# Recurrent gates of a Griffin encoder: both input parts stacked along the rows, gate halves moved by transfers

## The chip, the cores and the metric

The kernel runs on one core of a Trainium2 chip. The metric is the device time of one execution in microseconds (us). Times of a kernel are medians of several runs; the profile is one further execution, taken with the hardware profiler.

TensorE (PE) multiplies, VectorE (DVE), ScalarE (ACT) and GpSimd (POOL) do the rest, and nearly all transfers are issued by one queue, SyncE's (SP). PE accumulates into PSUM, which has eight banks of 128 x 512 float32 here.

## What is computed

Two layers, each a half-step FFN, a mixer, and a second half-step FFN, over 512 tokens of width 1024. The mixer projects once and runs attention beside a recurrent branch; the change touches the gates of that branch alone:

```python
def rg_lru(x, wa, ba, wx, bx, lam, reverse):
    xb = x.reshape(b, s, N_RNN_BLOCKS, RNN_BLOCK)             # 16 blocks of 64 channels
    r = sigmoid(einsum('bsnc,ncd->bsnd', xb, wa) + ba)
    i = sigmoid(einsum('bsnc,ncd->bsnd', xb, wx) + bx)
    log_a = -LRU_C * r * softplus(-lam)
    a = exp(log_a)
    u = sqrt(-expm1(2.0 * log_a)) * (i * x)
    _, h = associative_scan(_lin_combine, (a, u), axis=1, reverse=reverse)
    return h

hr = rg_lru(xc, ..., False) + rg_lru(xc, ..., True)           # xc: the convolved input
rnn = (hr * gelu(yr)) @ w_rnn_o
```

Every weight matrix of a gate is block diagonal: 16 blocks of 64 x 64 per gate and direction.

## The kernel before, in words

**Precision.** Every product of two float32 operands is built from float32r parts. An operand is split into a high part (ACT copies it to float32r) and a low part (DVE subtracts), and `mm3` (line 320) adds three matmuls: high by high, low by high, high by low.

**Layout.** Channels lie on partitions, tokens (512) along the free dimension. 1024 channels are eight tiles c = 0 to 7 of 128 channels, so that a tile holds two 64-channel blocks of the recurrence.

**Order.** The order is written by hand. `mix_ops` (line 176) lists the mixer's operations; `step()` (line 143) ticks a program clock, once per six matmuls in most operations, and `later(n, f)` puts the instructions of f into the engines' queues n ticks on. An engine runs its queue in order and waits only for its data, so a lag sets who stands ahead of whom and is no delay in itself. Every tick may also start a unit of attention (`unit`, line 732: two score banks, softmax, and two transposing DMAs of the probabilities on SP); a `pv` (line 783) follows every fourth unit.

**Weights.** `next_w()` (line 311) hands out weight chunks (128 x 512 float32, a gate's chunk 128 x 256) in program order. Its load goes out about ten chunks ahead on SP, its split into high and low about six chunks ahead on ACT and DVE. Chunks named in `EARLY` are split long before they are needed: `presplit` (line 231), during the layer's first FFN, loads a chunk, splits it, and writes both parts to the DRAM buffer `lsave`, from where `load_to` (line 279) later fetches both parts ready for use. It starts at tick `EARLY_AT[0]` of that FFN and takes a new chunk every `EARLY_AT[1]` ticks. Before, 72 chunks of each layer go this way, and the gates' chunks (`lru0`, `lru1`) do not.

**The recurrence.** `conv` (line 848) makes the tile `xc` and its parts `xh` (ACT) and `xl` (DVE). `lru(c, d)` (line 875), for direction d, takes two PSUM banks, one per gate: bank 0 for r, bank 1 for i, each `mm3` of a 128 x 128 weight with two 64 x 64 blocks on its diagonal. That is six matmuls and one tick. `tr` takes the tanh of each bank into the tiles `tr` and `ti` (one ACT instruction each, which frees the bank); `de` makes the decay `a` and the tanh of r on ACT and multiplies i by `xc` on DVE. After the second direction `rt` takes the square roots and `recur` (line 909) runs products, scans, sum and split. `R_LAGS` holds the lags: tr 1, de 2, rt 5. The last tile, c = 7, is the last that the output projection of the branch (`rnn`) waits for.

All SBUF work tiles come from one pool of 95 tiles.

Of the kernel before, what the change touches and what calls it, by code (L numbers as in the profile page):

```python
# [9 lines left out]
F32R = mybir.dt.float32r  # L10
F16 = mybir.dt.float16
ACTF = mybir.ActivationFunctionType
ALU = mybir.AluOpType
# [5 lines left out]
KD = D // 128  # L19
# [11 lines left out]
GELU_K = 0.7978845608028654  # L31
GELU_C = 0.044715


KC = 4

# [11 lines left out]
G_LAGS = (1, 2, 4, 6)  # L48
U_LAGS = (1, 5, 7, 9, 11, 14)
R_LAGS = (1, 2, 5, 1, 2, 6, 9, 13, 15)  # L50
GATES_1 = (1, 1, 1, 1, 1, 0, 0, 0)
GATES_2 = (1, 1, 1, 1, 1, 1, 0, 0)
GATES_3 = 1
# [8 lines left out]

EARLY = {"gA": 8, "gB": 8, "yr": 8, "xr": 8, "ao": 8}
EARLY_AT = (30, 3)
RATES = {"kv": 0.0, "q": 0.33, "xr": 0.33, "gA": 0.33, "gB": 0.33, "yr": 0.33, "lru0": 0.3, "lru1": 0.3, "rnn": 0.6, "aoa": 0.6, "ao": 0.0, "wk": 0.0, "wo": 0.0}


# [1 line left out]
def tile_griffin_encoder(  # L71
# [19 lines left out]
    V, A, G, SP, PE = nc.vector, nc.scalar, nc.gpsimd, nc.sync, nc.tensor  # L91
# [15 lines left out]
    def T(p, dtype=F32, shape=(128, 512)):  # L107
        return pool.tile(list(shape), dtype, name=nm(p), tag="T")

    def PS():  # L110
        return psp.tile([128, 512], F32, name=nm("ps"), tag="ps")
# [4 lines left out]
    def act(out, in_, func, **kw):  # L116
        A.activation(out, in_, func, **kw)  # L117

    def tt(out, a, b, op):
        V.tensor_tensor(out=out, in0=a, in1=b, op=op)  # L120
# [10 lines left out]
    def f32(ap):  # L131
        return ap.bitcast(F32)
# [6 lines left out]
    def later(n, fn):  # L139
        clock[1] += 1  # L140
        heapq.heappush(pend, (clock[0] + n, clock[1], fn))
# [13 lines left out]
    chunks = []  # L155
# [75 lines left out]
    def presplit(l, t0, dt):  # L231

        for n, i in enumerate(early[l]):
            st = {}

            def ld(i=i, st=st):
                ap, cols = chunks[i]
                st["w"] = T("er")
                SP.dma_start(out=st["w"].rearrange("p (a b) -> p a b", a=ap.shape[1]), in_=ap)

            def hi(st=st):
                st["h"] = T("eh", F32R)
                act(st["h"], st["w"], ACTF.Copy)

            def lo(st=st):
                tt(st["w"], st["w"], f32(st["h"]), ALU.subtract)

            def out(i=i, n=n, st=st):
                SP.dma_start(out=lsave[n, 0], in_=f32(st["h"]))
                SP.dma_start(out=lsave[n, 1], in_=st["w"])  # L250
                lows[i] = (lsave[n, 0], lsave[n, 1])

            for d, f in ((0, ld), (5, hi), (6, lo), (9, out)):
                later(t0 + n * dt + d, f)
# [24 lines left out]
    def load_to(n):  # L279
        while pos[0] < min(n, len(chunks)):  # L280
            ap, cols = chunks[pos[0]]
            if pos[0] in lows:
                hl = T("wh", F32R), T("wl", F32R)
                for t, src in zip(hl, lows[pos[0]]):
                    SP.dma_start(out=f32(t), in_=src)
                loaded[pos[0]] = hl
            else:
                t = T("wr")
                dst = t[:, 0:cols]
                if len(ap.shape) == 3:  # L290
                    dst = dst.rearrange("p (a b) -> p a b", a=ap.shape[1])
                SP.dma_start(out=dst, in_=ap)
                loaded[pos[0]] = t
            pos[0] += 1
# [25 lines left out]
    def mm3(ps, wh, wl, xh, xl, start, stop):  # L320
        PE.matmul(ps, wh, xh, start=start, stop=False)  # L321
        PE.matmul(ps, wh, xl, start=False, stop=False)  # L322
        PE.matmul(ps, wl, xh, start=False, stop=stop)  # L323
# [225 lines left out]
    def mix(l, norm, v, on_x):  # L549
        p = prm_t[l]  # L550
        hb, hc, nhc, sc, tb = v["hb"], v["hc"], v["nhc"], v["sc"], v["tb"]
        h = norm.h
# [295 lines left out]
        def conv(c, ps):  # L848
            st = rst[c] = {}
            xc = T("xc")  # L850
            st["xc"] = xc

            def w(j):
                return p[:, P_CW + 4 * c + j:P_CW + 4 * c + j + 1]

            act(xc, ps, ACTF.Identity, scale=w(2), bias=p[:, P_CB + c:P_CB + c + 1])

            def cj(o, i, j):
                stt(xc[:, o], ps[:, i], w(j), xc[:, o], ALU.mult, ALU.add)

            def ch():
                st["xh"] = T("xh", F32R)
                act(st["xh"], xc, ACTF.Copy)

            def cl():
                st["xl"] = T("xl", F32R)
                tt(st["xl"], xc, f32(st["xh"]), ALU.subtract)

            later(1, lambda: cj(slice(2, S), slice(0, S - 2), 0))
            later(1, lambda: cj(slice(1, S), slice(0, S - 1), 1))  # L870
            later(2, lambda: cj(slice(0, S - 1), slice(1, S), 3))
            later(3, ch)
            later(4, cl)

        def lru(c, d):
            st = rst[c]
            wh, wl = next_w()
            ps = []
            for g in range(2):
                ps.append(PS())  # L880
                sl = slice(g * 128, (g + 1) * 128)
                mm3(ps[g], wh[:, sl], wl[:, sl], st["xh"], st["xl"], True, True)
            step()
            j = d * 8 + c

            def tr():
                for n, q in enumerate(("r", "i")):
                    t = st[q, d] = T("t" + q)
                    act(t, ps[n], ACTF.Tanh, scale=0.5, bias=hb[:, 16 * n + j:16 * n + j + 1])

            def de():
                a, r = T("a"), st["r", d]
                st["a", d] = a
                act(a, r, ACTF.Exp, scale=hc[:, j:j + 1], bias=hc[:, j:j + 1])
                act(r, r, ACTF.Tanh, scale=nhc[:, j:j + 1], bias=nhc[:, j:j + 1])
                stt(st["i", d], st["i", d], 1.0, st["xc"], ALU.add, ALU.mult)

            later(R_LAGS[0], tr)
            later(R_LAGS[1], de)
            if d == 1:  # L900

                def rt():
                    for e in range(2):
                        act(st["r", e], st["r", e], ACTF.Sqrt, scale=0.25)

                later(R_LAGS[2], rt)
                recur(c, R_LAGS[2])

        def recur(c, t0):
            st = rst[c]  # L910
# [215 lines left out]
def _layout(inputs):  # L1126
    import numpy as np

    i = {k: np.asarray(v) for k, v in inputs.items()}

    def mtiles(w):
        l, k, m = w.shape
        return w.reshape(l, k // 128, 128, m // 128, 128).transpose(0, 3, 2, 1, 4)

    def vec(v):
        l = v.shape[0]
        return v.reshape(l, -1, 128).transpose(0, 2, 1)

    nl = i["w_in"].shape[0]
    w_in = i["w_in"]  # L1140
    kv = w_in[:, :, 1024:1536]
    qkv = np.stack([kv, w_in[:, :, 0:512], w_in[:, :, 512:1024]], 1)
    qkv = qkv.reshape(nl, 3, 8, 128, 512)
    lw = np.zeros((nl, 8, 128, 4, 128), w_in.dtype)
    for d in range(2):
        for g, w in enumerate((i["lru_wa"], i["lru_wx"])):
            for b in range(2):
                lw[:, :, b * 64:(b + 1) * 64, 2 * d + g, b * 64:(b + 1) * 64] = w[:, d, b::2]
    cw = i["conv_w"].reshape(nl, 4, 8, 128).transpose(0, 3, 2, 1).reshape(nl, 128, 32)
    rep = lambda a: np.broadcast_to(a[:, None, :], (nl, 128, a.shape[-1]))  # L1150
    prm = np.concatenate([
        vec(i["ffn1_norm"]), vec(i["mix_norm"]), vec(i["ffn2_norm"]), cw, vec(i["conv_b"]),
        vec(i["lru_ba"]), vec(i["lru_bx"]), vec(i["lru_lambda"]), vec(i["b_gate"]),
        rep(i["q_norm"]), rep(i["k_norm"])], 2)
    f4 = np.float32
    row = np.repeat(np.arange(8), 64).astype(f4)
    col = np.tile(np.arange(64), 8).astype(f4)
    inv = (f4(10000.0) ** (-np.arange(0, 32, 2, dtype=f4) / f4(32))).astype(f4)
    ar, ac = row[:, None] * inv, col[:, None] * inv
    cr, sr, cc, sc = np.cos(ar), np.sin(ar), np.cos(ac), np.sin(ac)  # L1160
    rope = np.stack([np.concatenate([cr, cr, cc, cc], 1), np.concatenate([-sr, sr, -sc, sc], 1)])
    rope = rope.reshape(2, 4, 128, 64).transpose(2, 0, 1, 3).astype(f4)
    out = {
        "xT": i["x"][0].T.reshape(8, 128, 512),
        "w1a": mtiles(i["ffn1_w1"]), "w2a": mtiles(i["ffn1_w2"]),
        "w1b": mtiles(i["ffn2_w1"]), "w2b": mtiles(i["ffn2_w2"]),
        "wqkv": qkv, "wfm": mtiles(w_in[:, :, 1536:]),
        "wao": mtiles(i["w_attn_o"]), "wro": mtiles(i["w_rnn_o"]), "wout": mtiles(i["w_out"]),
        "lruw": lw, "prm": prm, "rope": rope, "ident": np.eye(128, dtype=f4),
    }  # L1170
    return {k: np.ascontiguousarray(v) for k, v in out.items()}
# [20 lines left out]
```

## Time and profile before

| | us |
|---|---|
| median of 3 runs | 2345.41 (2345.22 to 2345.53) |
| the profiled execution, its own time | 2346.23 |
| its span, first to last instruction | 2344.4 |
| PE busy in it | 2337.9 |
| DVE busy | 1482.4 |
| ACT busy | 1065.0 |

The granted clock of PE is 1.0 of full speed in all of the span. In layer 0 the first FFN runs until some 367 us, the mixer until some 815 us; the gates' matmuls (`lru`) stand between 470 and 640 us. Layer 1 repeats this some 1166 us later. A matmul's end is modelled in the profile, so the durations of neighbours overlap; the time that one costs is read from the distance of two starts.

### The profile page before, as it was taken

What the parts mean: (1) busy time and instruction counts of PE and PEld (TensorE: products, weight loads), DVE (VectorE), ACT (ScalarE), POOL (GpSimd) and SP (SyncE); (2) the same over time, 40 slices, a digit from 0 to 9 for tenths busy, and PEclk for the clock granted to TensorE, in tenths of its full rate; (3) what the DMA queues carried; (4) which work ended last, traced back from release to release, by engine and by line L of the source; (5) the groups of instructions that cost most, each with busy time, mean ns of one, the idle gap of its engine ahead of it and who ended that gap; (6) DMA issues with size and microseconds to landing.
All of it is one profiled execution on the core that took longest, in us unless ns stands there. A gap on an engine that the chain in (4) does not pass through costs nothing.

```text
span 2344.4 us, 31489 instructions
## 1 busy us (share of the span) xinstructions
PE 2337.9 (100%) x10844; PEld 1905.3 (81%) x10844; DVE 1482.4 (63%) x2378; ACT 1065.0 (45%) x1942; POOL 239.9 (10%) x285
## 2 busy tenths in 40 slices
PE   9999999999999999999999999999999999999999
PEld 7888888877778888888888888888777788888887
DVE  7766756797975665553366767567878756655521
ACT  5443444577853333322234434445769534332321
POOL 1000000022331200000000000000223312000000
PEclk9999999999999999999999999999999999999999
DMA  5887895698789322233338878857988893222331
GB/s 188 291 274 258 295 303 189 191 236 223 205 206 256 121 90 86 86 95 99 116 101 296 276 258 310 276 162 209 249 206 198 206 277 100 90 86 86 95 104 63
DMA packets 382865, 436.83 MB, mean 186 GB/s; under 512 B 185328, under 2 KB 194416, under 8 KB 382704
## 3 DMA queue, kind: packets, MB, share of 16 engines
q1 hardware_dynamic: 382272, 434.68, 62.3%
q8 instruction: 85, 1.39, 0.2%
q14 instruction: 76, 0.62, 0.1%
q10 hardware_dynamic: 432, 0.14, 0.0%
HBM read 304.68 MB, written 90.18 MB: 168 GB/s over the span
## 4 chain that ended last, share of the span: by engine, by line
PE 98%; DVE 1%; ACT 0%; issue 0%; DMA 0%; ACTq 0%
PE ps L321 29%; PE ps L322 29%; PE ps L323 29%; PE ps L743 2%; PE ps L792 2%; PE ps L816 2%; PE ps L815 2%; PE ps L817 2%; DVE t L120 0%; DVE stk L120 0%; DMA wr<-in_w1a_dram 0%; DVE tr L123 0%; ACT p L117 0%; DVE pH L123 0%; ACT L117 0%
## 5 line engine op out<-in xcount | busy, mean ns | idle before, releaser
L120 DVE TENSOR_TENSOR wl<-wr,wh 128x512 fp32r<-128x512 f32 (+2 forms) x706 | 483.6, 708 | 183.2 <-ACT wh L117 146.8
L321 PE MATMUL ps<-hh,wh 128*128 128x512 f32 x1408 | 548.9, 390 | 0.5 <-ACT hh L117 0.5
L322 PE MATMUL ps<-hl,wh 128*128 128x512 f32 x1408 | 548.8, 390 | 0.0
L323 PE MATMUL ps<-hh,wl 128*128 128x512 f32 x1408 | 548.4, 390 | 0.0
L117 ACT ACTIVATE wh<-wr 128x512 fp32r<-128x512 f32 (+2 forms) x706 | 400.3, 598 | 123.5 <-DMA wr<-in_w2b_dram 68.8
L321 PEld LDWEIGHTS ps<-hh,wh 128*128 128x128 f32 x1408 | 264.8, 188 | 56.5 <-ACT hh L117 1.2
L322 PEld LDWEIGHTS ps<-hl,wh 128*128 128x128 f32 x1408 | 264.8, 188 | 55.5 <-DVE hl L123 0.5
L323 PEld LDWEIGHTS ps<-hh,wl 128*128 128x128 f32 x1408 | 264.8, 188 | 55.0
L321 PE MATMUL ps<-ah,wh 128*128 128x512 f32 x704 | 273.9, 389 | 0.0
L322 PE MATMUL ps<-al,wh 128*128 128x512 f32 x704 | 273.9, 389 | 0.0
L323 PE MATMUL ps<-ah,wl 128*128 128x512 f32 x704 | 273.9, 389 | 0.0
L321 PE MATMUL ps<-hnh,wh 128*128 128x512 f32 x512 | 207.1, 405 | 1.1 <-ACT p L117 1.1
L117 ACT ACTIVATE ah<-u 128x512 fp32r<-128x512 f32 x88 | 55.6, 632 | 318.5 <-DVE u L120 316.3
L322 PE MATMUL ps<-hnl,wh 128*128 128x512 f32 x512 | 199.9, 390 | 0.0
L323 PE MATMUL ps<-hnh,wl 128*128 128x512 f32 x512 | 199.9, 390 | 0.0
L126 POOL TENSOR_TENSOR sq<-sq,sq 128x512 f32<-128x512 f32 x42 | 57.2, 1362 | 1104.3 <-ACT sq L117 1103.8
L323 PEld LDWEIGHTS ps<-ah,wl 128*128 128x128 f32 x704 | 132.1, 188 | 27.6
L322 PEld LDWEIGHTS ps<-al,wh 128*128 128x128 f32 x704 | 132.1, 188 | 27.4
L321 PEld LDWEIGHTS ps<-ah,wh 128*128 128x128 f32 x704 | 132.1, 188 | 27.4
L117 ACT ACTIVATE th<-g 128x512 f32<-128x512 f32 x88 | 55.5, 632 | 213.8 <-DVE g L120 209.6
L123 DVE SCALAR_TENSOR_TENSOR x<-ps,x 128x512 f32<-128x512 f32 x48 | 32.9, 685 | 153.7 <-PE ps L323 153.7
L120 DVE TENSOR_TENSOR u<-ps,R 128x512 f32<-128x512 f32 x88 | 60.6, 689 | 109.5 <-PE ps L323 106.3
(160 smaller groups left out, 3433.9 us busy)
## 6 DMA issues: line engine op xcount, KB each, us to landing
wr<-in_w1b_dram SPq DMA_DIRECT2D x176, 256.0 KB, 2.6
wr<-in_w1a_dram SPq DMA_DIRECT2D x174, 256.0 KB, 4.4
lsave<-eh SPq DMA_DIRECT2D x144, 256.0 KB, 4.4
lsave<-er SPq DMA_DIRECT2D x144, 256.0 KB, 4.1
wh<-lsave SPq DMA_DIRECT2D x144, 256.0 KB, 3.8
wl<-lsave SPq DMA_DIRECT2D x144, 256.0 KB, 4.1
er<-in_wfm_dram SPq DMA_DIRECT2D x128, 256.0 KB, 4.7
wr<-in_w2a_dram SPq DMA_DIRECT2D x80, 256.0 KB, 5.0
```

The source lines that it names most:

```text
L117: A.activation(out, in_, func, **kw)
L120: V.tensor_tensor(out=out, in0=a, in1=b, op=op)
L123: V.scalar_tensor_tensor(out=out, in0=a, scalar=s, in1=b, op0=op0, op1=op1)
L126: G.tensor_tensor(out=out, in0=a, in1=b, op=op)
L321: PE.matmul(ps, wh, xh, start=start, stop=False)
L322: PE.matmul(ps, wh, xl, start=False, stop=False)
L323: PE.matmul(ps, wl, xh, start=False, stop=stop)
L743: PE.matmul(ps[ti].rearrange("p (t k) -> p t k", t=4), q[:, head % 8, :], kT[:, :, 2 * kv + j, :], start=j == 0, stop=j == 1)
L792: PE.matmul(po[hi * 64:(hi + 1) * 64, hf * 256:(hf + 1) * 256], vv[:, kt, kv * HD:(kv + 1) * HD], pt[hf][hi][o][:, :, kt, :], start=i == 0 ...
L815: PE.matmul(ps[t], hh[:, ts_], wh, start=k == 0, stop=False)
L816: PE.matmul(ps[t], hh[:, ts_], wl, start=False, stop=False)
L817: PE.matmul(ps[t], hl[:, ts_], wh, start=False, stop=k == KD - 1)
```

## The change: what it does

The input of the gates is stacked: for each of the two 64-channel blocks b of a tile there is one tile `xs[b]` whose rows hold the high part of the block in one half of the partitions and its low part in the other. The weight has the same 64 x 64 block in both row halves, and its columns hold gate r (first 64) and gate i (last 64). One matmul with the weight's high part and one with its low part then give the whole product of a block, both gates in one bank: four matmuls for two blocks instead of six for two gates.

A bank now holds one block with both gates, so the halves of r and i lie on the wrong partitions for half of the channels. For c = 0 to 6 `tr` reads each bank out whole into a tile `tg`, and `mv`, two ticks later, brings the four halves to their place by four SBUF-to-SBUF transfers of 64 x 512 on SP; `de`, `rt` and `recur` come five ticks later than before. For c = 7 (`direct`) `tr` itself writes the halves to their partitions in four half-height ACT instructions, and the lags stay. `ch` and `cl` become two half-height instructions each.

Beside that, the gates' chunks of both directions join `EARLY`, the last gA tile (two chunks) leaves it, and `presplit` starts at tick 14 instead of 30 with a chunk every 2.75 ticks instead of 3. 86 chunks of a layer go through `lsave`, 16 of them of half size.

```diff
+HALF = (slice(0, 64), slice(64, 128))
+MV_LAGS = (2, 5)
-EARLY = {"gA": 8, "gB": 8, "yr": 8, "xr": 8, "ao": 8}
-EARLY_AT = (30, 3)
+EARLY = {"gA": 7, "gB": 8, "yr": 8, "xr": 8, "lru0": 8, "lru1": 8, "ao": 8}
+EARLY_AT = (14, 2.75)
...
             def ch():
-                st["xh"] = T("xh", F32R)
-                act(st["xh"], xc, ACTF.Copy)
+                st["xs"] = [T("xs", F32R) for _ in range(2)]
+                for b in range(2):
+                    act(st["xs"][b][HALF[b]], xc[HALF[b]], ACTF.Copy)
             def cl():
-                st["xl"] = T("xl", F32R)
-                tt(st["xl"], xc, f32(st["xh"]), ALU.subtract)
+                for b in range(2):
+                    xs = st["xs"][b]
+                    tt(xs[HALF[1 - b]], xc[HALF[b]], f32(xs[HALF[b]]), ALU.subtract)
...
-            ps = []
-            for g in range(2):
-                ps.append(PS())
-                sl = slice(g * 128, (g + 1) * 128)
-                mm3(ps[g], wh[:, sl], wl[:, sl], st["xh"], st["xl"], True, True)
+            ps = [PS() for _ in range(2)]
+            for b in range(2):
+                sl = slice(b * 128, (b + 1) * 128)
+                PE.matmul(ps[b], wh[:, sl], st["xs"][b], start=True, stop=False)
+                PE.matmul(ps[b], wl[:, sl], st["xs"][b], start=False, stop=True)
             step()
...
+            direct = c == KD - 1
+            tg = []
             def tr():
+                if direct:
+                    for n, q in enumerate(("r", "i")):
+                        t = st[q, d] = T("t" + q)
+                        for b in range(2):
+                            col = 16 * b + j
+                            act(t[HALF[b]], ps[b][HALF[n]], ACTF.Tanh, scale=0.5, bias=hb[HALF[n], col:col + 1])
+                    return
+                for b in range(2):
+                    t = T("tg")
+                    act(t, ps[b], ACTF.Tanh, scale=0.5, bias=hb[:, 16 * b + j:16 * b + j + 1])
+                    tg.append(t)
+            def mv():
                 for n, q in enumerate(("r", "i")):
                     t = st[q, d] = T("t" + q)
-                    act(t, ps[n], ACTF.Tanh, scale=0.5, bias=hb[:, 16 * n + j:16 * n + j + 1])
+                    for b in range(2):
+                        SP.dma_start(out=t[HALF[b]], in_=tg[b][HALF[n]])
...
+            wait = 0 if direct else MV_LAGS[1]
             later(R_LAGS[0], tr)
-            later(R_LAGS[1], de)
+            if not direct:
+                later(R_LAGS[0] + MV_LAGS[0], mv)
+            later(R_LAGS[1] + wait, de)
...
-                later(R_LAGS[2], rt)
-                recur(c, R_LAGS[2])
+                later(R_LAGS[2] + wait, rt)
+                recur(c, R_LAGS[2] + wait)
```

`presplit` and `load_to` take a chunk's own width, and the host lays out the gates' weights and biases for the stacked form.

## Rows read from the trace of the kernel before

**Rows 1.** Page, part 1: engine, busy us (share of the span), instructions.

```profile
PE 2337.9 (100%) x10844; PEld 1905.3 (81%) x10844; DVE 1482.4 (63%) x2378; ACT 1065.0 (45%) x1942; POOL 239.9 (10%) x285
```

**Rows 2.** Waits of PE, whole span: waited for, us in total, times, longest.

```profile
PE ps L1087 <- POOL idle L1073: 1.3, 1, 1.3
PE ps L321 <- ACT p L117: 1.1, 2, 0.6
PE ps L321 <- ACT hh L117: 0.5, 1, 0.5
```

**Rows 3.** Timeline of PE, one `lru` of c = 3: start us, us, engine, operation.

```profile
558.47 0.39 PE L321 MATMUL ps<-xh,wh 128*128 128x512 f32 x1
558.69 0.40 PE L322 MATMUL ps<-xl,wh 128*128 128x512 f32 x1
...
559.84 0.39 PE L321 MATMUL ps<-hnh,wh 128*128 128x512 f32 x1
```

**Rows 4.** Groups of instructions, 352 to 740 us (mixer of layer 0): busy us, mean ns.

```profile
L321 PE MATMUL ps<-xh,wh 128*128 128x512 f32 x32 | 13.2, 411 | 0.0
L117 ACT ACTIVATE ti<-ps,hb 128x512 f32<-128x512 f32 x16 | 11.0, 687 | 0.1
L120 DVE TENSOR_TENSOR wl<-wr,wh 128x256 fp32r<-128x256 f32 x17 | 9.9, 582 | 8.4 <-ACT wh L117 8.4
L117 ACT ACTIVATE wh<-wr 128x256 fp32r<-128x256 f32 x17 | 6.9, 406 | 2.8 <-PE ps L323 1.8 <-DMA wr<-in_lruw_dram 1.0
L120 DVE TENSOR_TENSOR xl<-xc,xh 128x512 fp32r<-128x512 f32 x8 | 6.1, 762 | 0.0
L117 ACT ACTIVATE xh<-xc 128x512 fp32r<-128x512 f32 x8 | 5.0, 631 | 13.5 <-DVE xc L123 13.5
```

**Rows 5.** Timeline of PE, the matmul after `lru0` of c = 1, with its wait.

```profile
499.23 0.50 PE L321 MATMUL ps<-hnh,wh 128*128 128x512 f32 x1 [0.53 <-ACT p L117]
```

**Rows 6.** Windows: stretch; busy us of PE, PEld, DVE, ACT, POOL; clock; DMA; GB/s.

```profile
40.00:60.00 20.00, 20.00 (x90) 16.53 (x90) 16.60 (x27) 7.79 (x14) 0.00 (x0) 1.00 0.05 15
60.00:120.00 60.00, 60.00 (x266) 49.71 (x265) 44.89 (x71) 28.89 (x54) 0.00 (x0) 1.00 0.88 302
...
480.00:540.00 60.00, 59.47 (x297) 46.19 (x296) 52.33 (x82) 42.89 (x79) 16.29 (x22) 1.00 1.02 246
540.00:600.00 60.00, 60.00 (x336) 46.95 (x335) 43.79 (x69) 43.76 (x80) 17.51 (x23) 1.00 0.79 208
600.00:660.00 60.00, 60.00 (x301) 47.00 (x300) 55.81 (x82) 53.32 (x93) 23.09 (x26) 1.00 0.75 186
```

**Rows 7.** Windows again, last line: ten stretches of 20 us, 460 to 660 us.

```profile
sum 200.00, PE 199.47 PEld 155.80 DVE 169.16 ACT 156.44 POOL 61.48; mean PE 19.95 PEld 15.58 DVE 16.92 ACT 15.64 POOL 6.15
```

**Rows 8.** Timeline of SP: load of the chunk that Rows 3 uses.

```profile
527.12 0.38 SPq L292 DMA_DIRECT2D wr<-in_lruw_dram  x1
```

**Rows 9.** DMA view: issues of the gates' weights, KB each, median us to landing.

```profile
wr<-in_lruw_dram SPq DMA_DIRECT2D x32, 128.0 KB, 3.4
```

**Rows 10.** Tile PT (transposed probabilities), 480 to 600 us: its landings.

```profile
DMA to landing us min/median/max: 3.0/4.0/6.4
```

**Rows 11.** Waits of SP's queue, 480 to 680 us: us in total, times, longest.

```profile
SPq L771 <- DVE pH L123: 23.9, 10, 5.5
```

**Rows 12.** Timeline: end of c = 7's chain on DVE, and `rnn`'s first matmul on PE.

```profile
665.52 1.05 DVE L120 TENSOR_TENSOR rl<-tr,rh 128x512 fp32r<-128x512 f32 x1
...
667.86 0.58 PE L321 MATMUL ps<-rh,wh 128*128 128x512 f32 x1
```

More of the change, by code (lines that the diff above doesn't have):

```diff
@@ L237, in ld, with hi @@
                 ap, cols = chunks[i]
-                st["w"] = T("er")
+                st["w"] = T("er")[:, 0:cols]
                 SP.dma_start(out=st["w"].rearrange("p (a b) -> p a b", a=ap.shape[1]), in_=ap)
-            def hi(st=st):
-                st["h"] = T("eh", F32R)
+            def hi(st=st, cols=chunks[i][1]):
+                st["h"] = T("eh", F32R)[:, 0:cols]
                 act(st["h"], st["w"], ACTF.Copy)
@@ L246, in lo, with out @@
                 tt(st["w"], st["w"], f32(st["h"]), ALU.subtract)
[L248 to L251, printed above, removed]
+            def out(i=i, n=n, st=st, cols=chunks[i][1]):
+                dst = tuple(lsave[n, part][:, 0:cols] for part in range(2))
+                SP.dma_start(out=dst[0], in_=f32(st["h"]))
+                SP.dma_start(out=dst[1], in_=st["w"])
+                lows[i] = dst
             for d, f in ((0, ld), (5, hi), (6, lo), (9, out)):
@@ L284, in load_to @@
                 for t, src in zip(hl, lows[pos[0]]):
-                    SP.dma_start(out=f32(t), in_=src)
+                    SP.dma_start(out=f32(t)[:, 0:cols], in_=src)
                 loaded[pos[0]] = hl
@@ L1147, in _layout @@
             for b in range(2):
-                lw[:, :, b * 64:(b + 1) * 64, 2 * d + g, b * 64:(b + 1) * 64] = w[:, d, b::2]
+                for r in range(2):
+                    lw[:, :, r * 64:(r + 1) * 64, 2 * d + b, g * 64:(g + 1) * 64] = w[:, d, b::2]
     cw = i["conv_w"].reshape(nl, 4, 8, 128).transpose(0, 3, 2, 1).reshape(nl, 128, 32)
@@ L1152, in _layout @@
         vec(i["ffn1_norm"]), vec(i["mix_norm"]), vec(i["ffn2_norm"]), cw, vec(i["conv_b"]),
-        vec(i["lru_ba"]), vec(i["lru_bx"]), vec(i["lru_lambda"]), vec(i["b_gate"]),
+        *(np.concatenate([vec(i[n])[:, b * 64:(b + 1) * 64] for n in ("lru_ba", "lru_bx")], 1) for b in range(2)), vec(i["lru_lambda"]), vec(i["b_gate"]),
         rep(i["q_norm"]), rep(i["k_norm"])], 2)
```

## The prediction, made before the change was run

> **What bounds the kernel now.** I read the busy shares first, then who PE waits for, then PE's timeline, and only then the other engines in the stretch that the change touches. PE is busy in 2337.9 us of 2344.4, DVE in 63% and ACT in 45% [rows 1]. PE's own waits are three short entries, 2.9 us in all [rows 2]: two at the start, and two waits of about 0.55 us, one in each layer, for ACT to empty a bank. So the end is set by the number of matmuls times their cadence, and everything else counts only where it makes PE wait. The cadence is the distance of starts: from 558.47 to 559.84 us a gate operation puts six matmuls, 1.37 us, or 0.228 us each [rows 3] (the 0.39 us that a row gives as its length is modelled and overlaps the next one). That distance is the same for every full-size matmul here, and the weight load hides under it. The granted clock is 1.00 in each stretch that I list [rows 6], so there is no clock to win or lose.
>
> **What the change removes from PE.** A layer's mixer has 32 matmuls of each of the three kinds in the gates, 96 in all [rows 4]. Four instead of six per operation take away a third, 32 per layer and 64 in the kernel: 64 x 0.228 = 14.6 us. The new matmuls have the same shape (128 x 128 by 512, float32r), so I keep 0.228 us for them. If nothing else moved, the profiled execution would go from 2346.2 to 2331.6 us. It stands 0.8 us above the median of 2345.4, so on the median this is 2330.8 us. All further terms ask how much of the 14.6 us comes back as waiting.
>
> **ACT and DVE in the mixer.** Removed per layer: 16 splits of gate chunks, on ACT 16 x 0.406 = 6.5 us and on DVE 16 x 0.582 = 9.3 us [rows 4]; they move into the first FFN. Added per layer: `ch` is one more ACT instruction and `cl` one more DVE instruction per tile. No half-height instruction is in the trace; the bounds are half of the full one and all of it, 0.32 to 0.63 us and 0.38 to 0.76 us [rows 4]. I take the full ones, since the free size stays 512: ACT 8 x 0.63 = 5.0, DVE 8 x 0.76 = 6.1 us. `tr` keeps its two full instructions (0.69 us each [rows 4]); only c = 7 has two more per direction, 4 x 0.69 = 2.8 us on ACT. Together ACT gets 1.3 us more per layer and DVE 3.2 us less, of 156 and 169 us in the 200 us from 460 to 660 [rows 7]. That is nothing on the path by itself. But PE passes these 200 us 7.3 us sooner, so DVE goes from 169/200 = 85% to 166/193 = 86%, ACT from 78% to 82%.
>
> **Where PE touches the limit already.** After `lru0` of c = 1 PE waited 0.53 us for ACT [rows 5], inside the stretch where DVE is busy 52.3 of 60 us [rows 6]. Matmuls saved just before such a wait come back as a longer wait. Three gate operations (both of c = 0, the first of c = 1) lie before it, 3 x 0.46 = 1.4 us per layer at most; the last one alone, 0.46 us, at least. Bounds for two layers 0.9 and 2.7 us. I take 1.4, nearer the lower end, because the splits that leave ACT and DVE there give time back.
>
> **The transfers.** New on SP: per operation of c = 0 to 6 four issues, and one more load since a split chunk comes as two. An issue of 128 KB took 0.38 us [rows 8], so 5 x 0.4 = 2 us of SP per operation, 28 us per layer in some 150 us. Queued behind them on SP are weight loads and the attention's transposes. The loads have much room: the chunk used at 558.47 us was issued at 527.12 [rows 3, 8], 31 us ahead. The transposes wait already, up to 5.5 us for DVE [rows 11], and `pv` uses them six ticks (6 x 1.37 = 8.2 us) after the tick that issues them; two or three microseconds of SP do not show there.
>
> What can show is `de`. It now stands in ACT's queue behind four transfers, and if they are late, ACT stands still and the bank reads behind it with it. There is no row of an SBUF-to-SBUF transfer of 64 rows. The nearest are the gates' 128 KB load, 3.4 us to landing [rows 9], and the transposes, SBUF to SBUF, 3.0 to 6.4 us [rows 10]. With 4 x 0.4 us of issue the last half lands 4.6 to 8.0 us after `tr` if SP is free, and up to 5.5 us later if a transpose ahead of it waits [rows 11]. ACT gets to `de` five ticks later than before, about 5 x 1.37 = 6.8 us after `tr` where its queue is paced by PE. So the wait is 0 at one end and 8.0 + 5.5 - 6.8 = 6.7 us at the other. I take 1 us on average: 14 x 1 = 14 us per layer, against 200 - 156.4 = 43.6 us in which ACT is idle from 460 to 660 us [rows 7]. That is covered, but not everywhere: from 600 to 660 us only 6.7 of 60 us are free [rows 6]. I put 0.3 us of PE per layer on it, 0.6 in all. Without that cover each microsecond of mean wait would cost 14 us per layer.
>
> The transfers go through half of the partitions. In this trace all large loads span 128 partitions, and while the DMA engines were busy 1.02 of the time they moved 246 GB/s [rows 6]; nothing shows what 64 rows reach. [...]
>
> **DMA load.** From 480 to 540 us the DMA engines are busy all the time (1.02), from 540 to 660 us 0.75 to 0.79 [rows 6]. 512 KB of transfers and 128 KB of extra load per operation, at the 246 GB/s of the busy stretch, are 2.6 us; some four operations lie in the 60 us, so the work there is about 10 us too long and runs over into the next stretch, which has 60 x 0.21 = 12.6 us free. Loads 31 us ahead do not feel that.
>
> **The earlier split of chunks.** Before, 72 full chunks at one per 3 ticks; now 70 full and 16 half ones at one per 2.75, that is 78 full ones over 236 ticks, 0.330 per tick against 0.333. So the DMA rate of the first FFN (302 GB/s at 0.88 [rows 6]) stays, and only starts 16 ticks sooner. Seven chunks move into the time in which DVE works off the first banks; from 40 to 60 us DVE has 3.4 us free [rows 6], and seven subtractions of up to 0.76 us are 5.3 us. DVE falls about 2 us back there. With eight banks, each filled in 24 matmuls (5.5 us), PE does not meet that; if it did, it would be 2 us once. I take 0, bounds 0 and 2.
>
> **The end of the recurrence.** c = 7's last part ended at 666.57 and `rnn` began at 667.86, needing c = 7 only after 21 matmuls (4.8 us) [rows 12]: 6 us of room, of which c = 7's four extra ACT instructions take 2.8. For c = 0 to 6 five ticks more end before c = 7 does. Cost 0.
>
> **Sum.** 14.6 - 1.4 - 0.6 = 12.6 us. Profiled execution 2346.2 - 12.6 = 2333.6; median 2345.4 - 12.6 = 2332.8 us. With the bounds (cost 0.9 to 2.7, 0 to 1, 0 to 2) 2331.7 to 2336.5; if even the smallest cost is not met, 2330.8.
>
> **Rivals.** (a) *The readers become the bound.* From 480 to 540 and from 600 to 660 us DVE is busy 52.3 and 55.8 of 60 us [rows 6]. If PE cannot get ahead of DVE and ACT there, what 12 of a layer's 16 gate operations save turns into bank waits: 2 x 12 x 0.46 = 11 us lost, 3.6 us left, 2341.8 us. Against it: PE waited only twice in all [rows 2], and DVE loses work. (b) *Late transfers, slower than before.* The mechanism is `de` in ACT's queue. ACT has 43.6 us free per layer for 14 waits [rows 7]; it gains nothing when 2 x (14 w - 43.6) = 14.6, a mean wait w of 3.6 us. At 5 us, about the longest wait that SP shows ahead of a transpose [rows 11], it is 2 x (70 - 43.6) = 53 us, 2345.4 - 14.6 + 53 = 2384 us. For it: SP is crowded and the landings are up to 6.4 us [rows 10, 11]. Against it: five ticks of room and a landing of 3.4 us for the same size [rows 9]. (c) *The first FFN gives some back*, two to five microseconds from the earlier split work in both layers: 2335 to 2338 us. That the matmuls do not go away is no rival; the code issues four.
>
> **How the numbers follow.** The forecast holds with 0.72 (2330.8 to 2335), (c) with 0.07, (a) with 0.12, (b) with 0.09. The range from 2330.3 to 2338.5 holds the forecast, (c) and a little of (a), 0.8 in all, and leaves out most of (a) and all of (b). A measurement of this kernel can tell about 0.2% from no change, 4.7 us: faster means below 2340.7. That is the forecast, (c) and about four tenths of (a): 0.84; same is most of the rest of (a), 0.07; slower is (b), 0.09.
>
> **What the profile after would show.** PE with 64 matmuls fewer (10780), still busy in all but some 8 us of the span, and cadence 0.228 us in the gates. Waits of PE on ACT or DVE of about 2 us more in all, the largest near 480 to 500 us. `de` waiting for DMA for some 10 to 30 us in all. Wrong would be: waits of PE of over 8 us in the mixer with DVE at 95% or more in the stretches listed (a), or long ACT waits for the transfers that are followed by PE waits (b), or new PE waits before 367 us (c).

## The result, and the profile after

The change makes the kernel slower: 2381.76 us (2378.46 to 2383.30) against 2345.31 us, a ratio of 1.0151 [1.0139, 1.0163], or 36.4 us. The profiled execution took 2383.3 us, its span is 2381.5 us. One execution of the run `moves_only` below had a granted clock of 0.62 from end to end and took 3549 us; it is left out of that run's time.

The page of the changed kernel, busy time of each engine, beside [rows 1]:

```profile
PE 2338.3 (98%) x10780; PEld 1898.9 (80%) x10780; DVE 1499.4 (63%) x2394; ACT 1084.2 (46%) x1966; POOL 244.0 (10%) x285
```

The 64 matmuls are gone, and yet PE is as long busy as before, in a span 37 us longer. Where PE stood is in its waits over the whole span of the changed kernel (waited for, us in total, times, longest), beside [rows 2]:

```profile
PE ps L325 <- ACT tg L120: 14.3, 4, 4.1
PE ps L747 <- DVE y L126: 8.7, 2, 5.5
PE ps L325 <- ACT p L120: 8.5, 6, 2.3
PE ps L796 <- DMA PT<-pH: 4.4, 2, 2.3
PE ps L325 <- DVE y L126: 1.8, 2, 0.9
PE ps L1117 <- POOL idle L1103: 1.3, 1, 1.3
PE ps L889 <- DVE y L126: 0.5, 1, 0.5
```

Without the 1.3 us at the start these are 38.2 us; before, there were 1.1 us in the mixer. All of them lie in the two mixers. The same three stretches as in [rows 6], of the changed kernel (stretch; busy us of PE, PEld, DVE, ACT, POOL; clock; DMA; GB/s):

```profile
480.00:540.00 60.00, 56.56 (x282) 43.43 (x282) 46.03 (x70) 40.40 (x72) 14.66 (x19) 1.00 1.07 265
540.00:600.00 60.00, 56.28 (x309) 43.31 (x308) 42.65 (x65) 40.33 (x70) 16.49 (x22) 0.97 1.08 251
600.00:660.00 60.00, 51.94 (x248) 38.83 (x246) 42.20 (x65) 46.80 (x77) 14.77 (x19) 0.94 0.90 233
```

Three things to see. The DMA engines are full for 120 us instead of 60 (before 1.02, 0.79, 0.75). PE, DVE and ACT are all *less* busy than before, so none of them became the bound. And the granted clock, 1.00 before in all of these, is 0.97 and 0.94 in the last two. The timeline of PE in the changed kernel shows why, after its wait at 614.88 us (start us, us):

```profile
614.88 0.79 PE L325 MATMUL ps<-hnh,wh 128*128 128x512 f32 x1 [4.13 <-ACT tg L120]
615.47 0.63 PE L326 MATMUL ps<-hnl,wh 128*128 128x512 f32 x1
615.90 0.63 PE L327 MATMUL ps<-hnh,wl 128*128 128x512 f32 x1
...
618.57 0.40 PE L325 MATMUL ps<-hnh,wh 128*128 128x512 f32 x1
618.80 0.40 PE L326 MATMUL ps<-hnl,wh 128*128 128x512 f32 x1
```

PE had stood for 4.13 us, and the starts behind that are 0.43 us apart instead of 0.23: the granted clock is 0.50 of full speed from 614.9 to 618.1 us. Later they are back at 0.23. In the whole span the granted clock is 0.50 in six such stretches, 23.8 us together, in which 40 matmuls go at that distance, 40 x 0.20 = 8.0 us on top of the waits. Sum: 37.1 us more waiting, 8.0 us of lower clock, an estimated 6 us around the waits (some 0.3 us at each, since the matmuls just before and after one start further apart: at the wait of 1.17 us before 498.43 us the starts are 1.56 us apart, and the next two 0.33), less 14.6 us of matmuls: 36.5 us of the 37.

What the instructions behind the gates waited for in layer 0, 460 to 680 us, ACT and DVE of the changed kernel (us in total, times, longest; neither entry existed before):

```profile
ACT a L120 <- DMA tr<-tg: 25.8, 10, 6.9
...
DVE ti L126 <- DMA ti<-tg: 20.9, 6, 6.8
```

One of them can be followed to PE, in the timelines of DVE and PE at c = 3, second direction:

```profile
581.28 0.69 DVE L126 SCALAR_TENSOR_TENSOR ti<-ti,xc 128x512 f32<-128x512 f32 x1 [4.35 <-DMA ti<-tg]
...
586.65 0.68 DVE L126 SCALAR_TENSOR_TENSOR y<-y,ps 128x512 f32<-128x512 f32 x1
```

```profile
587.38 0.96 PE L747 MATMUL ps<-kT,qT 128*128 128x512 f16 x2 [3.21 <-DVE y L126]
```

DVE stood 4.35 us for i's halves and then worked without a pause until 587.33 us, when it let go of the bank for which PE had stood for 3.21 us.

SP's timeline says why the halves came late. The two banks of c = 2, second direction, were read out by 538.9 us; SP got to their transfers here (start us, us of the queue):

```profile
540.19 4.36 SPq L775 DMA_TRANSPOSE PT<-pH  x2
544.60 0.58 SPq L289 DMA_DIRECT2D wh<-lsave  x1
...
546.70 1.11 SPq L916 DMA_DIRECT2D tr<-tg  x2
547.87 1.52 SPq L916 DMA_DIRECT2D ti<-tg  x2
```

The transfers went out 7.8 us after the read, and SP was issuing for 6.5 us of that time: 4.36 us for two transposes, the rest for five weight loads. Added up over its timeline, SP spends 136 of the 160 us from 480 to 640 on issuing; before it was 96. Once issued, the transfers were no slower than supposed, as the DMA issues on the changed kernel's page show (KB each, median us to landing), beside the 3.4 us of [rows 9]:

```profile
tr<-tg SPq DMA_DIRECT2D x56, 128.0 KB, 3.6
ti<-tg SPq DMA_DIRECT2D x56, 128.0 KB, 3.3
```

### The profile page after: what moved, and what is told of

Read it like the earlier page. It is cut to its first block, busy times and chain, and to the rows that moved or that the text cites. A ratio compares the mean times of both kernels' runs of the same rounds, so it can differ in the third digit from the quotient of the medians.

```text
span 2381.5 us, 31828 instructions
## 1 busy us (share of the span) xinstructions
PE 2338.3 (98%) x10780; PEld 1898.9 (80%) x10780; DVE 1499.4 (63%) x2394; ACT 1084.2 (46%) x1966; POOL 244.0 (10%) x285
## 3 DMA queue, kind: packets, MB, share of 16 engines
q8 instruction: 84, 1.38, 0.2%
## 5 line engine op out<-in xcount | busy, mean ns | idle before, releaser
L123 DVE TENSOR_TENSOR wl<-wr,wh 128x512 fp32r<-128x512 f32 (+2 forms) x678 | 472.2, 720 | 201.8 <-ACT wh L120 166.8
L120 ACT ACTIVATE wh<-wr 128x512 fp32r<-128x512 f32 (+2 forms) x678 | 392.0, 608 | 140.9 <-DMA wr<-in_w2b_dram 69.1
L325 PEld LDWEIGHTS ps<-hnh,wh 128*128 128x128 f32 x512 | 97.9, 191 | 52.3 <-ACT tg L120 16.0
```

## The experiments

Diffs are against the changed kernel, except for `moves_only` and `early_only`, which start from the kernel before. Each ratio is to the kernel before, measured beside it.

**No transfers at all.** Every tile goes the way of c = 7: four half-height reads, old lags.

```diff
-            direct = c == KD - 1
+            direct = True
```

> The changed kernel without the transfers: every tile takes the path of c = 7, four half-height ACT instructions per gate operation that write the halves to their partitions, and the old lags. Theory T (the transfers are late because SP issues them late, and de holds ACT and DVE behind them): the waits of ACT and DVE for tg transfers, 46.7 us in layer 0, are gone, PE waits stay under 5 us, and the time is 2331 to 2338 us, the 14.6 us of matmuls less what 28 x 2 more ACT instructions of 0.68 us per layer-pair cost where ACT is full. Rival R1 (ACT and DVE are the bound once PE is shorter): PE waits for ACT of 10 us and more, 2341 us or over. Rival R2 (the extra loads and the earlier split cost the time): over 2360 us as with the change.

Measured: 2349.65 us, 1.0017 [1.0008, 1.0027]. Without the transfers and their delay 32 of the 36 us are gone. But the gain doesn't appear either: 2349.65 us is in the range of R1, not of T. The largest entry of its waits of PE:

```profile
PE ps L325 <- ACT ti L120: 11.8, 4, 4.2
```

In each layer PE waits 1.7 us at c = 5 and 4.2 us at c = 6, where no other operation stands between the two directions (the last two entries of `GATES_2` are 0), so that eight half-height reads come close together; ACT is busy 57.91 of the 60 us from 600 to 660 us. At c = 6 two table loads and the square roots of c = 5 stand ahead of these reads as well, from 612.34 to 617.08 us on ACT, so the reads alone don't account for that wait.

**Transfers and delay on the kernel before.** Six matmuls, the old early list, each gate's bank moved in two halves that stay on their partitions.

```diff
+                    t = T("t" + q if direct else "tg")
...
+                        SP.dma_start(out=t[HALF[b]], in_=tg[n][HALF[b]])
...
+            wait = 0 if direct else MV_LAGS[1]
```

> The kernel before with its six matmuls per gate operation and its old list of early chunks, plus the four transfers and the five ticks of delay of the change; each half is moved to the partitions it already has, so the result is the reference's. T: PE waits of 40 to 55 us come without any stacking, 2385 to 2400 us. R1: nothing is shorter on PE, so nothing becomes a bound: 2345 to 2350 us. R2: 2345 to 2352 us, since the extra loads are not there.

Measured: 2365.54 us, from one execution, between the ranges of T and of R1 and R2. The same kernel again:

> The kernel before plus the transfers and their delay, a second time, for its profile. Ts: SP issues over 120 us of the 160 us from 480 to 640 us; PE waits of 15 to 30 us in all, for DMA of PT, ACT and DVE; 2360 to 2370 us.

Measured: 2365.53 us, 1.0084 [1.0055, 1.0113]. Transfers and delay cost 19.5 us on the old kernel and 45.7 on the stacked one (below). I read this as PE reaching the same late banks sooner when it has less to multiply; no run shows it by itself. `a` waited only 8.3 us for transfers here (460 to 680 us), and PE still 12.7 us in the whole span for ACT to read `tg`. That was the first sign that lateness of the transfers is not all of it.

**Only r is moved**, i is taken as it lies in the second bank's tile, so half of i's values are those of r.

```diff
                 for n, q in enumerate(("r", "i")):
+                    if n == 1:
+                        st[q, d] = tg[1]
+                        continue
```

> The changed kernel with the transfers of r alone, two per gate operation; i is taken from the second bank's tile as it lies, so half of its values are those of r (this part of the computation is changed). T: SP has two issues less per operation and DVE no transfer to wait for, while ACT still waits for r: 2345 to 2362 us. R1 and R2: within 5 us of the change, 2377 to 2383 us.

Measured: 2364.96 us, 1.0082 [1.0062, 1.0102], a little above T's range. Leaving out half of the transfers, with the delay kept, gave back 17 of the 46 us.

**Only the early split of chunks** (the `EARLY` hunks alone on the kernel before).

> The kernel before with only the new list of early chunks (gate chunks split in the first FFN, start at tick 14, one per 2.75 ticks). T: no PE wait is added, 2344 to 2347 us. R2: a good part of the 37 us is here, over 2355 us.

Measured: 2344.37 us, 0.9994 [0.9985, 1.0004]: it costs nothing.

**No transfers and no delay**, banks read whole and taken as r and i as they lie.

```diff
-            direct = c == KD - 1
+            direct = True
...
+                for b, q in enumerate(("r", "i")):
+                    t = st[q, d] = T("tg")
+                    act(t, ps[b], ACTF.Tanh, scale=0.5, bias=hb[:, 16 * b + j:16 * b + j + 1])
```

> The changed kernel without transfers and without half-height reads: each bank is read out whole, as in the change, and its tile is taken for r or i as it lies (that part of the computation is changed), with the old lags. It has the stacked matmuls and the early split, and as many ACT instructions per operation as before. T (the forecast's sum, with the transfers as the step that failed): PE waits of under 4 us and 2330 to 2334 us. R1 (ACT and DVE are the bound as soon as PE is shorter, whatever reads the banks): 2340 us or over.

Measured: 2336.10 us, 0.9958 [0.9944, 0.9972]. This is what stacking is worth by itself: 9.9 us, with PE's waits in the mixers under 4 us as T has it and a time 2 us above T's range. The waits:

```profile
PE ps L325 <- ACT p L120: 2.4, 2, 1.2
PE ps L1109 <- POOL idle L1095: 1.3, 1, 1.3
PE ps L325 <- ACT tg L120: 1.1, 2, 0.6
```

**The delay alone**: that kernel, with `de`, `rt` and `recur` of c = 0 to 6 five ticks later. No transfer, no wait for one.

```diff
-            wait = 0 if direct else MV_LAGS[1]
+            wait = 0 if c == KD - 1 else MV_LAGS[1]
```

> The run without transfers (each bank's tile taken as r or i as it lies, that part of the computation changed), but with de, rt and recur of c = 0 to 6 five ticks later, as in the change. It is the control for the tiny transfers: those add four issues per operation to it and nothing else. Tu (the issues themselves cost the 21 us between the run without transfers and the run with tiny ones): within 4 us of the run without transfers, 2333 to 2340 us. Tv (the five ticks bunch ACT's and DVE's work behind c = 5 and 6, where PE waited 13 us for ACT in every run with the delay): 2348 to 2357 us.

Measured: 2351.75 us, 1.0028 [1.0018, 1.0038], 15.6 us above the one without delay and in Tv's range. Two timelines of ACT, at c = 5, show where a part of it comes from. First without the delay:

```profile
592.29 1.28 ACT L120 ACT_TABLE_LOAD   x1
593.59 1.15 ACT L120 ACTIVATE tg<-tg 128x512 f32<-128x512 f32 x2
...
595.42 1.28 ACT L120 ACT_TABLE_LOAD   x1
...
599.56 1.26 ACT L120 ACTIVATE tg<-ps,hb 128x512 f32<-128x512 f32 x2
...
602.27 1.25 ACT L120 ACTIVATE tg<-ps,hb 128x512 f32<-128x512 f32 x2
```

And with it:

```profile
600.41 1.28 ACT L120 ACT_TABLE_LOAD   x1
601.71 1.15 ACT L120 ACTIVATE tg<-tg 128x512 f32<-128x512 f32 x2
602.88 1.28 ACT L120 ACT_TABLE_LOAD   x1
604.17 2.42 ACT L120 ACTIVATE tg<-ps,hb 128x512 f32<-128x512 f32 x4
```

`tg<-ps` reads the banks; `tg<-tg` are the square roots of `rt`, and each batch has one table load of 1.28 us ahead of it and one behind. Without the delay the roots of c = 4 and both loads are over at 596.70 us, before PE fills the banks of c = 5 from 598.68 us on, and these are read at once. Five ticks later the roots of c = 4 come when PE has begun to fill the banks of c = 5 (from 599.42 us): four banks wait behind 3.8 us of table loads and roots. The timeline of PE in the kernel with the delay:

```profile
604.91 0.50 PE L325 MATMUL ps<-hnh,wh 128*128 128x512 f32 x1 [2.62 <-ACT tg L120]
```

That wait, once in each layer, is 5.2 us of the kernel's 15.5 us of waits behind its start; without the delay there were 3.8 us in all. The other waits that grew (5.8 us in all for `y` on DVE, the first long one 18 us further on, and `p` from 2.4 to 4.2) I have not followed to their start, so this order is shown for a part of the 15.6 us only. The changed kernel has the same order at the wait of 4.13 us shown above, as its timeline of ACT shows:

```profile
610.38 1.28 ACT L120 ACT_TABLE_LOAD   x1
611.68 1.15 ACT L120 ACTIVATE tr<-tr 128x512 f32<-128x512 f32 x2
612.85 1.28 ACT L120 ACT_TABLE_LOAD   x1
614.14 2.42 ACT L120 ACTIVATE tg<-ps,hb 128x512 f32<-128x512 f32 x4
```

The wait is 1.5 us longer there than with the delay alone. ACT had stood 1.92 us for a transfer of r until 605.14 us, and worked without a pause from there to these reads.

**Delay and issues, hardly any bytes**: four issues per operation as in the change, each of 64 rows of 64 bytes.

```diff
-                        SP.dma_start(out=t[HALF[b]], in_=tg[b][HALF[n]])
+                        SP.dma_start(out=tg[n][HALF[b], 0:16], in_=tiny[HALF[b]])
```

> The changed kernel with transfers that keep their number, their queue, their places and what waits for them, but carry 64 rows x 64 bytes of a constant instead of 64 rows x 2 KB (that part of the computation is changed; c = 7 reads its banks out whole as well). Ts (SP is full: each issue takes it 0.5 to 0.6 us, whatever it carries, and everything on SP gets late): 2365 to 2385 us, with SP issuing over 16 of 20 us from 480 to 640 us. Td (the bytes are the load, the DMA engines are full): 2336 to 2348 us.

Measured: 2357.25 us, 1.0049 [1.0026, 1.0072], between the two ranges; SP issuing 141 of the 160 us (106 with the delay alone). In a row, then: 2336.1 without transfers, + 15.6 for the delay, + 5.5 for the issues and the waits for their landing, + 24.5 for the bytes = 2381.8. The 5.5 us are near what these runs can tell (2355.8 to 2359.8 us against 2350.6 to 2354.2, and the two intervals overlap). The last step holds two more things: c = 7 is read whole in these kernels, and an operation holds two tiles of the pool where the change holds four. At the place followed to PE above, its wait for `y` is 0.22 us with the delay alone, 1.77 us with the tiny transfers and 3.21 us in the change.

**Other times and queues for the transfers.** Issued two ticks sooner; used twelve ticks later instead of five; on POOL's queue; on ACT's queue (both issued at once).

```diff
-MV_LAGS = (2, 5)
+MV_LAGS = (0, 5)
```

> The change with the transfers put into SP's queue two ticks earlier, at the tick of tr itself; de stays where it is. Ta (the transfers are late because of what stands ahead of them on SP): a good part of the waits goes, 2350 to 2372 us. Tb (SP is full as a whole, or the DMA engines are): 2375 to 2390 us.

Measured: 2384.72 us, 1.0166 [1.0146, 1.0186], with nearly the same waits: Tb. SP works through its queue; where in it the transfers stood by two ticks did not matter (2384.72 against 2381.76 us).

```diff
-MV_LAGS = (2, 5)
+MV_LAGS = (2, 12)
```

> The change with de, rt and recur twelve ticks later instead of five; the transfers are issued as before. Ta (de stands too early in the queues of ACT and DVE, and the waits there are the loss): the waits for tg nearly vanish, 2335 to 2350 us. Tb (the load on SP and the DMA engines costs the time, by late transposes and loads): 2365 us or over.

Measured: 2386.01 us, 1.0171 [1.0151, 1.0192]. This is Tb too. ACT hardly waits for the transfers any more, PE waits as long as in the change, now for others:

```profile
PE ps L796 <- DMA PT<-pH: 12.2, 4, 4.7
PE ps L326 <- DVE rl L123: 8.3, 2, 4.2
```

The 8.3 us are this experiment's own (c = 6 now ends after c = 7). The 12.2 us are the attention's transposes, which stand behind the transfers on SP and among them on the DMA engines. With the tiny transfers, as many on SP, PE had no wait for `PT`; so I put these down to the bytes.

```diff
-                        SP.dma_start(out=t[HALF[b]], in_=tg[b][HALF[n]])
+                        G.dma_start(out=t[HALF[b]], in_=tg[b][HALF[n]])
```

> The change with the four transfers issued from POOL's queue at the tick of tr instead of from SP's; same bytes, same DMA engines. Ts: SP falls back to about 110 us of issuing from 480 to 640 us, and unless POOL itself holds the attention's products back the time is 2340 to 2360 us. Td: 2370 to 2390 us.

> The change with the four transfers issued from ACT's queue right behind the two reads of the banks; same bytes, same DMA engines. Ts: SP is relieved as with POOL's queue, and if an issue costs ACT as little as SP's shortest, 2345 to 2365 us; if it costs ACT 0.5 us each, 28 us per layer, PE waits for ACT and it is 2370 us or more. Td: 2370 to 2390 us with long landings.

Measured: POOL 2386.12 us, 1.0172 [1.0126, 1.0218]; ACT 2405.1 us, 1.0253 [1.0220, 1.0286]. POOL's run is in Td's range, ACT's above both. With the transfers on ACT's queue SP is back at some 104 us of issuing, and nothing is won. With POOL's it still issues for 129 us, not 110: a transpose held it for 2.26 us there, on average, and for 1.71 in the change. The DMA issues of the kernel with POOL's queue:

```profile
wh<-lsave SPq DMA_DIRECT2D x140, 256.0 KB, 4.6
wl<-lsave SPq DMA_DIRECT2D x140, 256.0 KB, 4.9
tr<-tg POOLq DMA_DIRECT2D x56, 128.0 KB, 5.9
ti<-tg POOLq DMA_DIRECT2D x56, 128.0 KB, 7.3
```

I read this as follows: what no longer queued on SP queued in the DMA engines. The transfers land after 5.9 and 7.3 us instead of 3.6 and 3.3, weight loads take 0.8 to 0.9 us longer as well, and the busy share from 540 to 600 us is 1.11. Two rivals stay open. What POOL itself adds to such a landing was not measured apart, and on ACT an issue took 0.65 us on average (26.6 of the 160 us), time that its bank reads lack. With the same bytes none of the three queues has a median under 2381 us.

**Spreading the gate operations.** Two gate operations go from before the first direction of c = 2 and 3 to between the two directions of c = 5 and 6, first in the direct kernel, then in the changed one.

```diff
-GATES_1 = (1, 1, 1, 1, 1, 0, 0, 0)
-GATES_2 = (1, 1, 1, 1, 1, 1, 0, 0)
+GATES_1 = (1, 1, 1, 0, 0, 0, 0, 0)
+GATES_2 = (1, 1, 1, 1, 1, 1, 1, 1)
```

> No transfers, four half-height reads for every tile, and the gate projections spread so that one stands between the two gate operations of every tile (before, both operations of c = 5, 6 and 7 stood next to each other). In the run without transfers and without this spread, PE waited 11.8 us for ACT, all of it at c = 1, 5 and 6. T: these waits go with the bunching, 2332 to 2340 us. R1 (ACT has too much work in the mixer as a whole, 56 more instructions of 0.68 us): the waits only move, 2345 us or over.

Measured: 2338.26 us, 0.9967 [0.9954, 0.9980]. That is T's range: the entry of 11.8 us for `ti` is gone (the one for `p` grew from 1.2 to 4.8 us), and 11.4 us are won by an order alone.

> The whole change, with one gate projection between the two gate operations of every tile. Tw (a third of the loss is the bunching of two operations at c = 5, 6 and 7, where 8 transfers follow each other): 2362 to 2372 us. Tx (SP and the DMA engines are too full over the whole stretch, and spreading does not change their work): 2374 to 2385 us.

Measured: 2376.91 us, 1.0133 [1.0113, 1.0154]: 4.9 us, Tx's range. In the changed kernel the bunching is the smaller part. Its largest waits moved to another bank user:

```profile
PE ps L325 <- ACT p L120: 9.7, 5, 4.5
PE ps L747 <- ACT p L120: 6.7, 5, 2.4
PE ps L325 <- DVE y L126: 5.2, 2, 2.6
```

**The best version**: direct, spread, and `ch` taken from ACT to POOL.

```diff
-                    act(st["xs"][b][HALF[b]], xc[HALF[b]], ACTF.Copy)
+                    G.tensor_copy(out=st["xs"][b][HALF[b]], in_=xc[HALF[b]])
```

> The version without transfers, with half-height reads for every tile and the spread gate projections, and the two copies that make the high parts of xs moved from ACT to POOL, 16 x 0.63 = 10 us of ACT per layer less. If ACT's work from 460 to 600 us is what PE still waits for there (5.1 us): 2332 to 2337 us. [...]

Measured: 2334.39 us, 0.9953 [0.9938, 0.9967], 11.3 us faster than before and 47 us faster than the change. Its only waits of PE of a microsecond in the mixer are the two at c = 1:

```profile
PE ps L325 <- ACT p L120: 2.4, 2, 1.2
PE ps L1117 <- POOL idle L1103: 1.3, 1, 1.3
PE ps L889 <- ACT p L120: 1.0, 2, 0.5
```

## Why the prediction was wrong

It said 2332.8 us, and faster at 0.84. What came is the sign and nearly the number of its second rival (2384 us at a mean wait of 5 us), which had 0.09. The number is luck: the mean wait of `a` was 1.8 us, at which that rival's own formula gives no loss.

*Right.* The matmuls: stacked without transfers, the kernel was 9.9 us faster than the one before, measured beside it, where the first two terms, 14.6 - 1.4, gave 13.2. The wait at c = 1 grew as described, 1.22 us instead of the 0.53 of [rows 5]. Of the 3.3 us between, 1.0 are other short waits (3.5 us in the mixers against 1.1 before, where I took 1.4 more); the rest I have not followed. The early split: nothing. Half-height instructions cost about what full ones do (on DVE somewhat more, see the last section); groups of the changed kernel, 352 to 780 us (busy us, mean ns):

```profile
L123 DVE TENSOR_TENSOR xs<-xc,xs 64x512 fp32r<-64x512 f32 x16 | 13.9, 870 | 1.4 <-ACT xs L120 1.0
L120 ACT ACTIVATE xs<-xc 64x512 fp32r<-64x512 f32 x16 | 10.1, 628 | 5.8 <-DVE xc L126 4.1 <-issue 1.5
L120 ACT ACTIVATE ti<-ps,hb 64x512 f32<-64x512 f32 x4 | 2.7, 684 | 0.1
```

The landing of a transfer was right too: 64 rows of 2 KB landed in 3.3 to 3.6 us, the 128-row load of the same size in 3.4 [rows 9]. No run here sets 64 rows against 128 with the engines full.

*The step that failed* is "The transfers", at three places.

First, the cover. I set 14 waits of `de` against 43.6 us of ACT's idle time, summed over 200 us, and found the break-even at a mean wait of 3.6 us. `a` waited 25.8 us in 14 operations, 1.8 us each, half of the break-even, and the kernel lost 36 us. The waits of DVE for i, 20.9 us, are not in that sum at all, and the one followed to PE above is one of these. Nor does the sum of ACT's waits tell the loss: with the tiny transfers `a` still waited 17.9 us, at a cost of some 5.5 us, and with a lag of twelve ticks hardly at all, at the time of the change. Idle time was not saved up: there are eight banks, and where DVE stood for 4.35 us at c = 3, or four bank reads stood behind 3.8 us of table loads and roots on ACT, PE ran through them and stood too, for 3.21 and 4.13 us, although ACT was busy in only 40.33 of the 60 us from 540 to 600 us.

Second, the five ticks. I took them as room for the transfers and charged nothing ("Cost 0" in "The end of the recurrence"). They cost 15.6 us, a third of the 45.7, with no transfer in the kernel: what moves in an in-order queue stands ahead of something else, and where I followed it, for 5.2 us of the waits, it was two table loads and two square roots ahead of four bank reads. The rows to see that were in the trace of before, on ACT's own timeline; I asked how long `de` may wait and not what `rt` would then stand ahead of.

Third, SP's queue. I gave an issue 0.4 us and a transfer that waits behind a transpose up to 5.5 us. The issues of transfers took 0.56 to 0.61 us on average, a transpose 1.71 us instead of 1.38 (1.65 already without transfers), and an operation's four transfers were all issued 2 to 10 us after its banks were read. The mean wait became 1.8 us instead of the 1 us that I took; only the longest, 6.9 us, is at the upper end of 6.7.

*The other one* is "DMA load". I let the 10 us by which 480 to 540 us is overfull run into the free 12.6 us of the next stretch. But the additions go on in that stretch as well: 1.07, 1.08, 0.90. The step with the bytes is 24.5 us of the end, and neither an earlier issue nor another queue nor a longer lag takes it away. "Loads 31 us ahead do not feel that" was true of the weights; the transposes and the transfers are needed within 8 us and did feel it. And "no clock to win or lose" did not hold: the granted clock fell to 0.50 after PE's wait of 4.13 us, and over the kernel the lower clock cost 8.0 us.

The first rival (readers as the bound) is off for the change, with DVE at 42 to 46 of 60 us; in the direct kernel it came true, with ACT. The third (the first FFN) is off: PE has no new wait before 370 us.

Open: the waits for `y` on DVE under the delay alone, and how the bytes' 24.5 us divide between late transposes and late halves. Not tried: putting `rt` behind the next tile's reads with the transfers kept, and matmuls that write 64 of the output partitions each, so that both gates land where they belong (`pv` writes 64 at a time, the 128*64 matmuls of line 796).

## What to carry to other kernels

Don't cover a wait in an in-order queue with idle time summed over a stretch; ask what stands behind it, and how long the buffers (here eight banks) last the engine that is the bound. A longer lag was not free (five ticks cost 15.6 us here): list what the delayed steps, table loads among them, will now stand ahead of. And before adding transfers that are needed soon (here within 8 us), look how busy the DMA engines and their queue already are (here 1.02 from 480 to 540 us, and 96 of 160 us): reading a result twice in halves, with the work spread, took 2338.26 us here, and moving it, spread alike, 2376.91.

## What the runs showed of the hardware that I had not expected

- On ACT half-height and full copies are alike (628 against 631 ns). On DVE the half-height subtraction took 870 ns, the full one 762 [rows 4], but half of the partitions isn't the reason: over both layers, those during which POOL ran nothing took 687 ns on average (12 of 32), the full ones 682 (10 of 16), and those during which POOL also ran took 979 and 892. More of them met POOL in the changed kernel. Why they take longer then, no run here shows.
- A table load on ACT took 1.28 us, with the next instruction 0.02 us behind it; `rt` pays two for 1.15 us of work.
- After PE had stood for 4.13 us the granted clock was 0.50 of full speed from 614.9 to 618.1 us, 0.43 us a matmul instead of 0.23. Over the kernel the lower clock put 8.0 us on top of 38 us of waits.
- Issued on POOL or ACT instead of SP, 128 KB transfers landed later (5.9 and 7.3, or 4.3 and 5.1, against 3.6 and 3.3 us), with the busy share of the DMA engines at 1.11 from 540 to 600 us in both (1.08 on SP).
